# Gathered experts beside the late attention, and part of the dense experts' first products before the gates

## The chip, the cores and the metric

The kernel runs on one NeuronCore of a Trainium2 chip. The metric is the time of one launch on the device in microseconds (us); three runs of the kernel before gave 3617.83, 3618.16 and 3625.24, so the median is 3618.16.

## What is computed

One layer of a hybrid decoder, for 1024 prompt tokens (8 blocks of 128) and 32 sample tokens (8 sequences of 4 tokens, each with 2048 cached positions). A projection feeds an S5 state-space head group and latent attention; both are mixed and added to the input. Then comes PEER, a retrieval over 128 x 128 experts, which takes more than half of the time. Cut to that part:

```python
q = (xb @ wq).reshape(PEER_BLOCK, PEER_HEADS, 2, PEER_HALF)
s = jnp.einsum('qhcd,ckd->qhck', q, keys)
s1, i1 = lax.top_k(s[:, :, 0], PEER_TOPK)
s2, i2 = lax.top_k(s[:, :, 1], PEER_TOPK)
...
top, sel = lax.top_k(cand, PEER_TOPK)
idx = jnp.take_along_axis(cidx, sel, axis=-1)
g = jax.nn.softmax(top, axis=-1)
act = jax.nn.gelu(jnp.einsum('qhkd,qd->qhk', jnp.take(u_tab, idx, axis=0), xb))
return jnp.einsum('qhk,qhkd->qd', (g * act), jnp.take(v_tab, idx, axis=0))
```

Each token picks 128 of 16384 experts (8 heads x 16); expert number = first key x 128 + second key.

## The kernel before

The tokens are treated in two ways. Blocks 0 to 2 (`early`) and the sample block are *sparse*: `Sparse.block` gathers, slot by slot, 128 rows of `peer_u` (tile `pu`) by an indirect DMA from POOL, multiplies them with the tokens and sums them on DVE (`pact`), and later gathers `peer_v` rows (`pv`) and adds them into `pacc`. That is 2 x (3 x 128 + 32) = 832 gathers of 512 KB and as many DVE steps, with five row buffers (`RB`). Blocks 3 to 7 (`late`, 640 tokens, `TD`) are *dense*: every one of the 16384 experts is computed and weighted by a gate that is zero where the expert was not picked. `Gates` builds the gates in memory (`g_d`), 80 steps of 8 tokens; `Dense.group` then goes over the 128 second keys, four at a time: load and split `ur` into a high and a low part (`uh`, `ul`), 48 products of 320 columns (`da`, the first products), gelu, times the gate, split (`hh`, `hl`), and 30 products of 512 columns with the `peer_v` rows of that key (`dy`, `dres`).

Before that, in the program's order: S5 and projections; `attention` over all 64 units (block, head) with the 16 steps of `split_wq` (split the query weights and write them to `wq_d`) beside it; `mix_out` for all 8 blocks (`oz`); `score` for all 8 blocks (query products `rqp`, key products `rscp`, the best 16 by `top16` on DVE); `select` for the three early blocks, which makes the lists that the gathers need; then, in `rest`, `select` for the late blocks, the sample's attention (`Sample.run`: 8 sequences, key products `kk`, then `soften` and `gather`), the sample block's own mixing, scoring and selection between the gate steps, and the dense stage. `weave` puts the gathers between the steps of `rest`: each step yields a cost, cost x `PACE` is credit, and a gather step costs 1.5.

A scheduler of the language then reorders the instructions of each engine by its own estimate, within the dependencies and the buffers; each engine and each DMA queue (SP, ACT, POOL) then runs its list strictly in order. So sample work stands among the attention in the built program although it is written behind it.

Of the kernel before, what the change touches and what calls it, by code (L numbers as in the profile page):

```python
# [22 lines left out]
NB = 8  # L23
# [227 lines left out]
def build(ctx, nc, tc, a):  # L251
# [58 lines left out]
    xn_d = dram.tile([NT, D], F32, name="xn_d")  # L310
    g_d = dram.tile([NTB, 128, 128, TBLK], F32, name="g_d")
# [12 lines left out]
    es = ExitStack()  # L324
    with right():
        smp = Sample(es, nc, tc, a, ident, keep, o_d)
# [16 lines left out]
    sparse.open(ctx.enter_context(tc.tile_pool(name="ring", bufs=1)))
    er = ExitStack()
    slots = er.enter_context(tc.tile_pool(name="slots", bufs=1))
    i1T, wT = (slots.tile([128, TD], F32, name=nm) for nm in ("i1T", "wT"))
    i2T = slots.tile([128, TD], BF16, name="i2T")

    def take_dense(b, i1, i2, w, pool, pp):
        cs = slice((b - D0) * 128, (b - D0) * 128 + 128)  # L350
        tp = pp.tile([128, 3, 128], F32, name=f"slt{b}", tag="slt")
        for j, (src, dst) in enumerate(((i1, i1T), (i2, i2T), (w, wT))):
            nc.tensor.transpose(tp[:, j], src, ident)
            nc.scalar.copy(dst[:, cs], tp[:, j])

    e2 = ExitStack()
    pools = ranks(e2, nc, tc, a, "p")
    for b0, n in SSEL:
        select(nc, pools, early[b0 : b0 + n], tv[:, b0 : b0 + n], ti[:, b0 : b0 + n], sparse.take)

    def rest():

        for b0, n in DSEL:
            bs = slice(D0 + b0, D0 + b0 + n)
            select(nc, pools, late[b0 : b0 + n], tv[:, bs], ti[:, bs], take_dense)
            yield 25.0 * n
        e2.close()
        et.close()
        drive(smp.run())
# [1448 lines left out]
```

## Time and profile before

| what | value |
|---|---|
| median of three runs | 3618.16 us |
| the profiled execution: time / span | 3620.32 us / 3617.9 us |
| mean granted TensorE clock | 0.944 |
| PE busy | 3347.4 us, 93% |
| PEld (weight loads) busy | 2929.9 us, 81% |
| DVE / ACT / POOL busy | 2716.4 / 1156.2 / 1233.4 us |
| HBM traffic | 229 GB/s over the span |

The span is from the first to the last instruction; 2.4 us of the profiled time lie around it. PE's matmuls overlap each other, so its busy time is an upper reading of its work; start-to-start intervals in the timeline tell what one matmul really takes. The granted clock is a share of 2.4 GHz; 0.5 is 1.2 GHz.

### The profile page before, as it was taken

How to read it: one execution, taken by the hardware profiler on the slowest of the kernel's cores; microseconds unless marked ns; L12 is line 12 of the kernel's file. 1: busy time of each engine (PE TensorE's matmuls, PEld its weight loads, DVE VectorE, ACT ScalarE, POOL GpSimd, SP SyncE). 2: the span in 40 equal slices, each digit the busy share in tenths (PEclk: the TensorE clock that was granted, in tenths of full speed). 3: DMA queues.
4: the chain of work that ended last, by engine and by line, in shares of the span. 5: the costliest groups of instructions: out<-in, count | busy, mean ns of one | idle time of the engine just before them, and what ended most of it. 6: DMA issues, size and time to landing. Idle time of an engine off the chain costs nothing.

```text
span 3617.9 us, 52406 instructions
## 1 busy us (share of the span) xinstructions
PE 3347.4 (93%) x19464; PEld 2929.9 (81%) x19464; DVE 2716.4 (75%) x5777; ACT 1156.2 (32%) x2268; POOL 1233.4 (34%) x1044
## 2 busy tenths in 40 slices
PE   8899899999999634998799999999999999999999
PEld 7778687765799523987798898889988989998898
DVE  7674664434577998779688888888888888888884
ACT  4333454422322422456522121222222222222221
POOL 1020100000000104222155556555555556555551
PEclk9889799999999866778899999999999999999999
DMA  3335931143322207777899999999999999999992
GB/s 132 86 88 155 315 130 46 48 152 111 115 82 71 87 26 250 290 248 252 294 308 312 318 318 325 320 315 341 321 314 313 342 333 318 326 317 324 327 328 104
DMA packets 324606, 832.19 MB, mean 230 GB/s; under 512 B 36696, under 2 KB 150488, under 8 KB 313536
## 3 DMA queue, kind: packets, MB, share of 16 engines
q0 software_dynamic: 130608, 510.98, 39.9%
q1 hardware_dynamic: 92752, 247.75, 20.0%
q10 hardware_dynamic: 100992, 70.13, 6.7%
q8 instruction: 153, 2.51, 0.3%
q14 instruction: 101, 0.83, 0.1%
HBM read 734.44 MB, written 92.94 MB: 229 GB/s over the span
## 4 chain that ended last, share of the span: by engine, by line
PE 42%; issue 19%; POOL 13%; DMA 13%; DVE 11%; ACT 2%; SPq 0%; ACTq 0%; POOLq 0%; DVEq 0%
POOL pv L1335 9%; DMA pv<-in_peer_v_dram,idx 6%; POOL pu L1335 4%; PE gps L1219 4%; PE oz L1029 3%; DMA pu<-in_peer_u_dram,idx 2%; DVE pu L1349 2%; PE po L709 2%; PE s L688 2%; PE kk L139 2%; PE rqp L139 2%; PE rqp L140 2%; PE rqp L141 2%; PE kk L141 1%; PE kk L140 1%
## 5 line engine op out<-in xcount | busy, mean ns | idle before, releaser
L1335 POOL DMA_INDIRECT pu<-in_peer_u_dram,idx x384 | 522.6, 1361 | 618.3 <-DVE pact L1349 478.9
L1335 POOL DMA_INDIRECT pv<-in_peer_v_dram,idx x384 | 521.4, 1358 | 391.2 <-DVE pacc L1361 282.9
L139 PE MATMUL da<-xdh,uh 128*128 128x320 f32 x2048 | 636.8, 311 | 19.0 <-ACT ga L1292 18.7
L141 PE MATMUL da<-xdh,ul 128*128 128x320 f32 x2048 | 634.8, 310 | 2.3 <-DVE ul L129 2.3
L140 PE MATMUL da<-xdl,uh 128*128 128x320 f32 x2048 | 635.1, 310 | 0.0
L1361 DVE SCALAR_TENSOR_TENSOR pacc<-pv,pw,pacc 128x1024 f32<-128x1024 f32 x416 | 533.8, 1283 | 100.0 <-DMA pv<-in_peer_v_dram,idx 90.8
L1349 DVE CUSTOM_DVE_ANT_0 pu<-pu,pxn 128x1024 f32<-128x1024 f32 x416 | 496.7, 1221 | 90.2 <-DMA pu<-in_peer_u_dram,idx 82.5
L139 PEld LDWEIGHTS da<-xdh,uh 128*128 128x128 f32 x2048 | 387.1, 189 | 30.3 <-ACT ga L1292 23.5
L140 PEld LDWEIGHTS da<-xdl,uh 128*128 128x128 f32 x2048 | 387.1, 189 | 6.4
L141 PEld LDWEIGHTS da<-xdh,ul 128*128 128x128 f32 x2048 | 386.6, 189 | 6.3 <-DVE ul L129 2.8
L139 PE MATMUL dy<-vh,hh 128*128 128x512 f32 x768 | 302.5, 394 | 20.4 <-DVE yac L1308 20.4
L140 PE MATMUL dy<-vl,hh 128*128 128x512 f32 x768 | 299.8, 391 | 0.0
L141 PE MATMUL dy<-vh,hl 128*128 128x512 f32 x768 | 298.0, 390 | 0.0
L128 ACT CAST uh<-ur 128x1024 fp32r<-128x1024 f32 x128 | 134.5, 1051 | 394.3 <-PE da L140 391.3
L1292 ACT ACTIVATE ga<-da 128x320 f32<-128x320 f32 x256 | 110.0, 432 | 428.6 <-PE da L141 426.8
L1219 PE MATMUL gps<-hv,h 128*128 128x128 f32 x800 | 203.8, 415 | 23.8 <-DVE hv L1212 5.5
L128 ACT CAST vh<-vr 128x1024 fp32r<-128x1024 f32 x128 | 132.0, 1049 | 249.2 <-DMA vr<-in_peer_v_dram 180.0
L129 DVE TENSOR_TENSOR vl<-vr,vh 128x1024 fp32r<-128x1024 f32 x128 | 156.4, 1223 | 60.1 <-ACT vh L128 59.6
L1219 PEld LDWEIGHTS gps<-hv,h 128*128 128x128 f32 x800 | 168.8, 242 | 39.8 <-issue 16.4
L139 PE MATMUL dres<-vh,hh 128*128 128x512 f32 x512 | 200.5, 392 | 0.0
L140 PE MATMUL dres<-vl,hh 128*128 128x512 f32 x512 | 199.6, 392 | 0.0
L139 PEld LDWEIGHTS dy<-vh,hh 128*128 128x128 f32 x768 | 144.2, 188 | 54.5 <-DVE yac L1308 25.2
(528 smaller groups left out, 7148.1 us busy)
## 6 DMA issues: line engine op xcount, KB each, us to landing
ur<-in_ut_dram SPq DMA_DIRECT2D x128, 512.0 KB, 6.3
vr<-in_peer_v_dram SPq DMA_DIRECT2D x128, 512.0 KB, 6.5
g_d<-gbuf SPq DMA_DIRECT2D x20, 2048.0 KB, 7.6
gt<-g_d ACTq DMA_DIRECT2D x32, 1280.0 KB, 18.1
wq_d<-wq POOLq DMA_DIRECT2D x16, 1024.0 KB, 7.8
rwp<-wq_d POOLq DMA_DIRECT2D x16, 1024.0 KB, 5.1
rwn<-wq_d POOLq DMA_DIRECT2D x16, 1024.0 KB, 5.4
wqr<-in_peer_wq_dram SPq DMA_DIRECT2D x16, 512.0 KB
```

Of the source, the lines that this page charges most:

```text
L128: nc.scalar.copy(hi, raw)
L129: nc.vector.tensor_tensor(lo, raw, hi, OP.subtract)
L139: nc.tensor.matmul(out, ah, bh, start=(first and i == 0), stop=False)
L140: nc.tensor.matmul(out, ah, bl, start=False, stop=False)
L141: nc.tensor.matmul(out, al, bh, start=False, stop=(last and i == n - 1))
L688: nc.tensor.matmul(s[:, c0 : c0 + w], qT[:, h, :], kT[:, h, c0 : c0 + w], start=True, stop=c0 + w != nk)
L1029: nc.tensor.matmul(z[:n], cat[:, k, :n], w[:, k, hs], start=(k == 0), stop=(k == 7))
L1219: nc.tensor.matmul(ps[:, :, j - j0], h1[:, j], hv[:, :, j] if j < GV else ha[:, j - GV], start=True, stop=True)
L1292: nc.scalar.activation(ga[:, cs], ps[:, :HW], AF.Gelu_apprx_tanh)
L1335: self.nc.gpsimd.indirect_dma_start(out=r, out_offset=None, in_=self.a[table], in_offset=bass.IndirectOffsetOnAxis(ap=ix, axis=0))
L1349: nc.vector.tensor_tensor_reduce(ur, ur, xn, 1.0, 0.0, OP.mult, OP.add, act[:, s : s + 1])
L1361: nc.vector.scalar_tensor_tensor(acc, vr, w[:, s : s + 1], acc, OP.mult, OP.add)
```

## The change

Attention is still one generator over all blocks, but only the 24 units of the early blocks come first, with the 16 `split_wq` steps beside units 2 to 17. Mixing, scoring and selection of the three early blocks follow at once, and the gathers may start. The other 40 attention units, the mixing and scoring of the late blocks (the query weights and `w_out` are read once more) now stand in `rest`, with sample steps between them, and give credit for gathers. The gate steps give less credit (1.5 for 4.0), the dense steps too (2.16 for 2.35). New is `Ahead`: for 16 of the 128 second keys (7, 15, ... 127) the first products are made before the dense stage and written to `ad_d` in memory; the dense stage loads them (327,680 bytes a key) in place of `ur`, its split and 48 products. `Ahead` has one buffer of each kind. The diff, cut:

```diff
-    drive(attention(nc, tc, a, ident, qkv, o_d, early + late, lambda pool: split_wq(nc, a, pool, wq_d)))
-    drive(mix_out(nc, tc, a, gl_d, o_d, x1_d, xn_d, early + late, "e"))
...
-    drive(score(nc, tc, a, ident, xn_d, [(early, None), (late, xt)], lambda b: tv[:, b], lambda b: ti[:, b], "p", wq_d))
...
+    att = attention(nc, tc, a, ident, qkv, o_d, early + late)
+    next(att)
+    with right(), tc.tile_pool(name="wqs", bufs=2) as pool:
+        for _, _ in zip(split_wq(nc, a, pool, wq_d), range(16)):
+            next(att)
+    for _ in range(8 * D0 - 17):
+        next(att)
+    drive(mix_out(nc, tc, a, gl_d, o_d, x1_d, xn_d, early, "e", "right"))
+    with right(), ExitStack() as e1:
+        tv, ti = tops(e1, D0, "e")
+        drive(score(nc, tc, a, ident, xn_d, [(early, None)], lambda b: tv[:, b], lambda b: ti[:, b], "e", wq_d, 2, "right"))
+        pools = ranks(e1, nc, tc, a, "e")
+        for b0, n in SSEL:
+            select(nc, pools, early[b0 : b0 + n], tv[:, b0 : b0 + n], ti[:, b0 : b0 + n], sparse.take)
+    es = ExitStack()
+    with right():
+        smp = Sample(es, nc, tc, a, ident, keep, o_d)
...
+        short_att = smp.run()
...
+        for _ in beside(att, 1, ATT_FREE):
+            yield 15.0
+        for _ in beside(mix_out(nc, tc, a, gl_d, o_d, x1_d, xn_d, late, "d"), 2):
+            yield 40.0
...
+        for _ in beside(score(nc, tc, a, ident, xn_d, [(late, xt)], lambda b: tv[:, b - D0], lambda b: ti[:, b - D0], "d", wq_d), 1):
+            yield 5.0
+        ea = ExitStack()
+        ahead = Ahead(ea, nc, tc, a, xt, ad_d)
...
+                select(nc, pools, late[b0 : b0 + n], tv[:, bs], ti[:, bs], lambda *x: take_dense(dst3, *x))
+                for _ in range(3 * n):
+                    next(short_att, None)
         et.close()
-        drive(smp.run())
+        drive(short_att)
...
         for _ in gates:
-            yield GT * 0.5
+            yield 1.5
+        drive(ahead.run())
...
-DENSE_PACE = 2.35
+DENSE_PACE = 2.16
+ATT_FREE = 20
...
+AHEAD = list(range(7, 128, 8))
...
+class Ahead:
...
+        self.sp = es.enter_context(tc.tile_pool(name="ah", bufs=1))
+        self.pp = es.enter_context(tc.tile_pool(name="ahp", bufs=1, space=PSUM))
...
+        for n, i2 in enumerate(AHEAD):
+            ur = sp.tile([128, 8, 128], F32, name=f"aur{i2}", tag="ur")
+            nc.sync.dma_start(ur, self.a["ut"][i2])
+            uh = sp.tile([128, 8, 128], F32R, name=f"auh{i2}", tag="uh")
+            ul = sp.tile([128, 8, 128], F32R, name=f"aul{i2}", tag="ul")
+            split(nc, uh, ul, ur)
+            da = sp.tile([128, TD], F32, name=f"ada{i2}", tag="da")
+            for c0 in range(0, TD, HW):
+                cs = slice(c0, c0 + HW)
+                ps = self.pp.tile([128, 512], F32, name=f"aps{i2}_{c0}", tag="da")
+                mm3(nc, ps[:, :HW], [(uh[:, k], ul[:, k], xh[:, k, cs], xl[:, k, cs]) for k in range(8)])
+                nc.scalar.copy(da[:, cs], ps[:, :HW])
+            nc.sync.dma_start(self.ad_d[n], da)
...
+            if i2 in AHEAD:
+                nc.sync.dma_start(ga, self.ad_d[AHEAD.index(i2)])
+                nc.scalar.activation(ga, ga, AF.Gelu_apprx_tanh)
+            else:
```

What the scheduler makes of it, at three places. First DVE, where the sample's set-up stands (`qg`, `qTb`, `pidx`, `sukl`). Before, among the attention's maxima (`mx`) of the third block:

```order
L691 TENSOR_REDUCE mx_0_4806<-s_0_4803 128x1
L802 TENSOR_SCALAR qg<-qTs,gk 64x256
L815 COPY qTb<-qTs 96x256
L704 COPY pT_7_4810<-pt_7_0_4811 128x256
L691 TENSOR_REDUCE mx_1_4835<-s_1_4832 128x1
L723 TENSOR_TENSOR oT_4827<-oT_4827,po_4699 128x512
L691 TENSOR_REDUCE mx_2_4857<-s_2_4854 128x1
```

Now, straight behind the end of the early selection (`fi` and `idx` are the last early block's list; `pT_7` and `oT` belong to the last attention unit):

```order
L1393 SCALAR_TENSOR_TENSOR fi_6463<-kn_6443,kn_6453 128x128
L1394 CAST idx<-fi_6463 128x128
L831 TENSOR_SCALAR qg<-qTs,gk 64x256
L844 COPY qTb<-qTs 96x256
L736 COPY pT_7_8876<-pt_7_0_8877 128x512
L821 TENSOR_SCALAR pidx<-ptx 128x8
L822 TENSOR_TENSOR pidx<-pidx,ptx 128x8
L129 TENSOR_TENSOR sukl<-sukr,sukh 128x512
L129 TENSOR_TENSOR movl<-sukr,movh 128x2x256
```

The whole attention now stands ahead of the sample's set-up; before, half of the sample's work stood among it.

Second PE, around the last late selection (`slt` turns its results) and the first gate (`gps`). Before:

```order
L353 MATMUL slt_9676<-ident,re_9592 128x128
L353 MATMUL slt_9824<-ident,kn_9804 128x128
L353 MATMUL slt_9824<-ident,kn_9814 128x128
L353 MATMUL slt_9824<-ident,re_9765 128x128
L1070 MATMUL rtp_0_13998<-ident,rxn_13996 128x32 x4
L1070 MATMUL rtp_1_14005<-ident,rxn_13996 128x32 x4
L1219 MATMUL gps_0_13935<-hv_13927,h_0_13925 128x128 x4
L1219 MATMUL gps_4_13941<-hv_13927,h_0_13925 128x128
```

Now, the 768 products `aps` of `Ahead` stand among `kk` and `slt`, some 1100 rows ahead of the first gate:

```order
L141 MATMUL kk_1_0_11692<-sukh,sll_0_11526 128x256
L357 MATMUL slt_12729<-ident,kn_12684 128x128
L139 MATMUL aps_0_17069<-xdh,auh_17064 128x320
L140 MATMUL aps_0_17069<-xdl,auh_17064 128x320
...
L357 MATMUL slt_12729<-ident,kn_12703 128x128
...
L141 MATMUL aps_320_17095<-xdh,aul_17065 128x320
L357 MATMUL slt_13282<-ident,kn_13244 128x128
L139 MATMUL aps_0_17129<-xdh,auh_17124 128x320
L140 MATMUL aps_0_17129<-xdl,auh_17124 128x320
L141 MATMUL aps_0_17129<-xdh,aul_17125 128x320
```

Two keys follow each other there with one row between them, where the splits `auh` and `aul` have one buffer. The sample's last `kk` rows, `soften`, `gather` and `soa` stand behind the last `aps`, and the first `gps` behind them, as before.

Third SP's queue in the dense stage, where a key of `AHEAD` has its load:

```order
L1339 DMA vr_18450<-in_peer_v_dram 128x1024
L1339 DMA vr_18523<-in_peer_v_dram 128x1024
L1334 DMA ur_18792<-in_ut_dram 128x1024
L1339 DMA vr_18719<-in_peer_v_dram 128x1024
L1334 DMA ur_18868<-in_ut_dram 128x1024
L1339 DMA vr_18798<-in_peer_v_dram 128x1024
L1349 DMA ga_18531<-ad_d 128x640
L1334 DMA ur_18947<-in_ut_dram 128x1024
L1334 DMA ur_19196<-in_ut_dram 128x1024
```

`ga` is read back from memory in the same queue as `ur` and `vr`; in the kernel before nothing but those two stands here.

## Rows read from the trace of the kernel before

**Rows 1.** Stretches: start:end, length, busy PE PEld DVE ACT POOL, clock, DMA share, GB/s.
```profile
450.00:756.00 306.00, 305.04 (x2155) 242.33 (x2153) 157.69 (x276) 146.08 (x383) 11.78 (x21) 1.00 0.21 69
756.00:950.00 194.00, 181.37 (x811) 110.19 (x812) 73.97 (x211) 44.30 (x126) 6.91 (x12) 0.96 0.47 156
950.00:1180.00 230.00, 228.76 (x1589) 227.86 (x1588) 171.71 (x1027) 59.09 (x140) 7.99 (x15) 1.00 0.23 76
1180.00:1429.00 249.00, 111.29 (x692) 81.63 (x692) 235.43 (x1077) 78.67 (x166) 54.52 (x44) 0.70 0.35 118
1429.00:1640.00 211.00, 205.98 (x1111) 191.75 (x1112) 155.62 (x223) 106.63 (x231) 49.66 (x51) 0.77 0.73 262
1640.00:1783.00 143.00, 125.53 (x635) 117.05 (x633) 134.44 (x252) 91.18 (x188) 37.50 (x31) 0.86 0.75 269
1783.00:1812.00 29.00, 14.82 (x67) 14.55 (x68) 9.48 (x13) 7.29 (x10) 2.91 (x2) 0.66 0.87 275
1812.00:3618.00 1806.00, 1774.74 (x9875) 1607.10 (x9873) 1488.00 (x1758) 436.98 (x632) 1008.40 (x746) 1.00 0.90 312
```

**Rows 2.** Groups in 1180 to 1429 us: instructions, count, busy us, mean ns.
```profile
L1335 POOL DMA_INDIRECT pu<-in_peer_u_dram,idx x32 | 46.7, 1460 | 132.0 <-DVE pact L1349 106.8 <-DVE idx L1330 16.4 <-issue 6.7
L1349 DVE CUSTOM_DVE_ANT_0 pu<-pu,pxn 128x1024 f32<-128x1024 f32 x28 | 32.9, 1212 | 0.8 <-DMA pu<-in_peer_u_dram,idx 0.8
...
L880 DVE TENSOR_REDUCE ssq<-ssqr 128x8 f32<-128x512 f32 x28 | 18.9, 673 | 0.6 <-ACT ssqr L877 0.6
```

**Rows 3.** Timeline of PE, 2500 to 2506 us: start, us, instruction.
```profile
2499.95 0.32 PE L140 MATMUL da<-xdl,uh 128*128 128x320 f32 x1
...
2505.69 0.31 PE L140 MATMUL da<-xdl,uh 128*128 128x320 f32 x1
```

**Rows 4.** Timeline and chain that ended last: third attention block, the sample's set-up.
```profile
418.17 0.56 DVE L691 TENSOR_REDUCE mx<-s 128x1 f32<-128x384 f32 x1 [0.94 <-PE s L689]
...
416.98 14.54 DMA sukr<-in_w_uk_dram
437.99 2.12 PE qpp L808 x18
```

**Rows 5.** Tile wq and its write: ns min/median/max; KB, us from issue to landing.
```profile
L128 ACT CAST wq<-wqr x16: 1030/1050/1122, 368.6 to 488.7; 128x1024 fp32r<-128x1024 f32 x16
L129 DVE TENSOR_TENSOR wq<-wqr,wq x16: 1209/1216/1226, 371.0 to 490.3; 128x1024 fp32r<-128x1024 f32 x16
...
wq_d<-wq POOLq DMA_DIRECT2D x16, 1024.0 KB, 7.8
```

**Rows 6.** Timeline of PE in mixing and scoring; chain: products of one mixing block.
```profile
800.30 0.30 PE L140 MATMUL kk<-movl,slh 128*128 128x288 f32 x1
800.44 0.30 PE L141 MATMUL kk<-movh,sll 128*128 128x288 f32 x1
...
840.35 13.73 PE oz L1029 x32
...
1010.29 0.33 PE L141 MATMUL rqp<-rxhp,rwp 128*128 128x384 f32 x1
1010.46 0.61 PE L1091 MATMUL rscp<-keysp,rqTp 128*128 128x128 f32 x4
1010.82 0.42 PE L139 MATMUL rqp<-rxhp,rwp 128*128 128x384 f32 x1
```

**Rows 7.** Tile kk: first and last start.
```profile
L139 PE MATMUL kk<-sukh,slh x256: 277/282/682, 452.7 to 1284.8; 128*128 128x256 f32 x128
```

**Rows 8.** Groups in 1640 to 1783 us: gathered blocks on DVE.
```profile
L1349 DVE CUSTOM_DVE_ANT_0 pu<-pu,pxn 128x1024 f32<-128x1024 f32 x30 | 36.6, 1221 | 0.0
```

**Rows 9.** Stretches, tile pu (DVE, POOL, clock, DMA), then pacc (PE, PEld, DVE, POOL).
```profile
1812.00:3550.00 1738.00, 379.78 (x319) 438.07 (x316) 1.00 0.93 321
...
1812.00:3550.00 1738.00, 0.00 (x0) 0.00 (x0) 533.77 (x416) 3.87 (x6) 1.00 0.93 321
```

**Rows 10.** Waits in 1900 to 3400 us: us in total, times, longest.
```profile
DVE pacc L1361 <- DMA pv<-in_peer_v_dram,idx: 87.3, 79, 4.9
```

More of the change, by code (lines that the diff above doesn't have):

```diff
@@ L310, in build @@
     xn_d = dram.tile([NT, D], F32, name="xn_d")
+    ad_d = dram.tile([len(AHEAD), 128, TD], F32, name="ad_d")
     g_d = dram.tile([NTB, 128, 128, TBLK], F32, name="g_d")
@@ L323, in build @@
     sparse = Sparse(nc, tc, a, hold, x1_d, xn_d)
-    es = ExitStack()
-    with right():
-        smp = Sample(es, nc, tc, a, ident, keep, o_d)
+    sparse.open(ctx.enter_context(tc.tile_pool(name="ring", bufs=1)))
     wq_d = dram.tile([16, 128, 2, 8, 128], F32R, name="wq_d")
@@ L343, in build @@
[L343 to L349, printed above, removed]
+    att = attention(nc, tc, a, ident, qkv, o_d, early + late)
[3 more added lines that the diff above has]
+            next(att)
@@ L357, in build, with beside @@
-    pools = ranks(e2, nc, tc, a, "p")
-    for b0, n in SSEL:
-        select(nc, pools, early[b0 : b0 + n], tv[:, b0 : b0 + n], ti[:, b0 : b0 + n], sparse.take)
     def rest():
[L363 to L367, printed above, removed]
+        short_att = smp.run()
+        def beside(steps, n, first=0):
+            for i, _ in enumerate(steps):
+                if i >= first:
+                    for _ in range(n):
+                        next(short_att, None)
+                    yield
@@ new lines, in rest @@
+        ea = ExitStack()
+        ahead = Ahead(ea, nc, tc, a, xt, ad_d)
+        er = ExitStack()
+        slots = er.enter_context(tc.tile_pool(name="slots", bufs=1))
+        i1T, wT = (slots.tile([128, TD], F32, name=nm) for nm in ("i1T", "wT"))
+        i2T = slots.tile([128, TD], BF16, name="i2T")
+        dst3 = i1T, i2T, wT
+        with ExitStack() as e2:
+            pools = ranks(e2, nc, tc, a, "d")
+            for b0, n in DSEL:
+                bs = slice(b0, b0 + n)
+                select(nc, pools, late[b0 : b0 + n], tv[:, bs], ti[:, bs], lambda *x: take_dense(dst3, *x))
+                for _ in range(3 * n):
+                    next(short_att, None)
@@ L388, in rest @@
                 if next(gates, 1) is None:
-                    yield GT * 0.5
+                    yield 1.5
         for _ in gates:
-            yield GT * 0.5
+            yield 1.5
+        drive(ahead.run())
         with right():
-            dense_mm = Dense(ctx, nc, tc, a, ident, xt, g_d, x1_d)
+            dense_mm = Dense(ctx, nc, tc, a, ident, xt, g_d, x1_d, ad_d)
         eb.close()
         er.close()
+        ea.close()
         sparse.pp = dense_mm.pa
@@ L661, in split_wq, with attention @@
         yield
-def attention(nc, tc, a, ident, qkv, o_d, blocks, job, side="left"):
+def attention(nc, tc, a, ident, qkv, o_d, blocks, side="left"):
     with ExitStack() as e1, ExitStack() as e2:
@@ L759, in attention @@
                 close(b, po, rss[b])
-            if b >= 2:
-                next(extra, None)
             yield 0.5 + 0.55 * (b + 1)
@@ L1272, in group @@
             i2 = j0 + j
-            ur = xp.tile([128, 8, 128], F32, name=f"ur{i2}", tag="raw", bufs=UB)
-            nc.sync.dma_start(ur, a["ut"][i2])
-            uh = xp.tile([128, 8, 128], F32R, name=f"uh{i2}", tag="uh")
-            ul = xp.tile([128, 8, 128], F32R, name=f"ul{i2}", tag="ul")
-            split(nc, uh, ul, ur)
+            if i2 not in AHEAD:
+                ur = xp.tile([128, 8, 128], F32, name=f"ur{i2}", tag="raw", bufs=UB)
+                nc.sync.dma_start(ur, a["ut"][i2])
+                uh = xp.tile([128, 8, 128], F32R, name=f"uh{i2}", tag="uh")
+                ul = xp.tile([128, 8, 128], F32R, name=f"ul{i2}", tag="ul")
+                split(nc, uh, ul, ur)
             vr = xp.tile([128, 1024], F32, name=f"vr{i2}", tag="vr", bufs=VB)
```

31 lines of the change are left out of this document (18 added, 13 removed).

## The prediction

> **What bounds the kernel now.** I read the busy times by stretch first, then the groups of the costly stretches, the timeline of PE and the waits. The stretches [rows 1] show four limits in turn. From 450 to 1180 us PE is busy for nearly all of the time: 305 of 306 us in the attention, 181 of 194 in the mixing, 229 of 230 in the scoring. From 1180 to 1429 us lies a hole: PE is busy for 111 of 249 us, its granted clock falls to 0.70 between its two levels, and DVE is busy for 235. Here the late selection, the last sample keys and the first 28 gathered blocks [rows 2] all stand on DVE. The gates follow in two parts, 1429 to 1640 with PE busy for 206 of 211 us, and 1640 to 1783 with DVE busy for 134 of 143. Last comes the dense stage, 1806 us with PE busy for 1775 at clock 1.00, so there a PE product that goes away is time that goes away. What one costs is not its busy time, since products overlap: 40 `da` products start between 2499.95 and 2505.69 us [rows 3], 39 intervals in 5.74 us, so 0.147 us each, where each row alone says 0.31.
>
> The change drops no PE work. 768 products leave the dense stage and are done before it. So a gain can only come from time in which PE stands or crawls, and that is 138 us in the hole, 13 in the mixing, 17 in the second half of the gates, and the slow clock of hole and gates.
>
> **Start to the sample's set-up (367 to 759).** Blocks 0 and 1 run as before: the third block's first maximum comes at 418.2 [rows 4], so 50 us, or 25 a block and 3.1 a unit. Beside units 2 to 17 stand the 16 `split_wq` steps. One step takes cast 1.05, difference 1.22 and write 7.8 us [rows 5]; with 1 for its load that is 11 us, and two buffers give one step per 5.5 us, 88 us from 402, so to 490. That is 73 past 417. By the order list the early mixing comes with one more attention block: 3 x 13.73 [rows 6] + 25 = 66. The early scoring is 16 pieces of 24 query products (start to start 1010.29 to 1010.46, 0.17) and six key products (four take 0.36, so 0.09 each) [rows 6], 4.7 us a piece and 75 in all, with five attention units (17) among them, and about 10 for `xn` through memory: 102. The early selection is DVE work. In the hole DVE is busy for 235, less 33 for `pu` and 19 for `ssq` [rows 2], which leaves 23 a block for eight blocks with some sample work in it, so I take 20: 60, and 13 attention units beside it whose maxima and copies DVE does in the same list, 41: 101. Sum 50 + 73 + 66 + 102 + 101 = 392, to 759. In the kernel before this point was passed at 417 and the sample's keys began at 452.7 [rows 7], since its set-up stood among the attention.
>
> **From the set-up to the first gate (759 to 1479; before, the first gate stood at 1429).** PE has here: `kk`, 256 of each of six kinds, 1536, at 0.13 from start to start (800.30 to 800.44 is 0.14) [rows 6, 7], 200; five mixing blocks of 13.73, 69; 768 late query products of 0.147, 113; 160 key products of 0.09, 14; the `aps`, 16 x 48 x 0.147 = 113; some 640 small ones (turns, `soften`, the sample's own block) at 0.09, 58: 567. DVE has about as much. By the order list 117 gathers stand ahead of the first gate where there were 28: 117 x 1.21 [rows 2] = 142. The late scoring has five eighths of the 172 us of [rows 1], 107. Five selections of 20 are 100; `ssq` 128 x 0.673 [rows 2] = 86, and 44 for the split of the latents; the 16 splits of `Ahead` at 1.22 [rows 5], 20; and 65 for the rest: 564. Two lists of that length that wait for each other don't run at 1.0. The share of PE was 0.99 in the scoring, 0.93 in the mixing, 0.45 in the hole [rows 1]; I take 0.9, nearest the mixing, since DVE was 38% busy there and will be fuller here: 630. The ends of this are 573 (0.99) and 709 (0.8). Two stretches come on top. The set-up has nothing on PE beside it now: `sukr` takes 14.5 us to land, then `qpp`, then keys; from 417 to 452.7 it was 36 with attention as cover [rows 4, 7], so 30 (0 if late attention still covers, 36 if not). And the sample's last chain (`soften`, `gather`, `soa`, mixing, scoring) stands behind the last `aps` and has no cover: 60. That makes 720, so to 1479, 50 later than before, with 113 of moved products and 108 of moved DVE steps inside.
>
> **Gates and ramp (333 + 29).** The first part is PE's, 211 as before. In the second DVE sets the pace with 30 gathered blocks [rows 8]. The gate steps now earn less credit, and some 32 gathers stand in the stage instead of 66; so 17 of those 30 go: 17 x 1.22 = 21 of 143, leaving 122. Nothing less, since DVE was busy for 134 there. Then 29 of ramp as before [rows 1]: 1479 + 333 + 29 = 1841.
>
> **Dense (1693).** 768 products x 0.147 = 113 less than 1806. It has 683 gathers for 735, so DVE, at 82%, isn't the next bound: 319 `pu` and 416 `pacc` were 380 and 534 us of it [rows 9]. DMA is the near one, at 0.90; 52 gathers of 512 KB and 16 x 190 KB fall away, 30 of 563 MB or 5%, against 6% of the time, so its share rises to 0.91. If that pace bound, the stage would lose 92, not 113. The loads of `ga` go through SP's queue behind `ur` and `vr`; each has the group's second products as cover (a group is 1806/32 = 56 us, its first products 4 x 48 x 0.147 = 28, so 28 are left), and if one comes late the nearest row is a wait of 4.9 us, the longest for `pv` [rows 10].
>
> **Sum.** 1841 + 1693 = 3534 of span; with 2.4 around it 3536.4 against 3620.3 of the profiled execution, 83.9 less. From the median 3618.16 that is 3534. The 1841 are 29 more than 1812. With the ends above (573 to 709 for 630, 92 for 113) this case's own range is 3480 to 3600.
>
> **Rivals.** *The hole closes wholly.* If DVE and PE interleave without loss, the 175 us in which PE is not busy between 450 and 1783 (length less busy, summed) [rows 1] go: 3620 - 175 = 3445. For it: attention, keys and gathers are independent and now stand together. Against: DVE is then as full as PE. The Trainium skill (Perfetto Trace Analysis, Identifying the Most-Contended Engine) says that matmul busy time is a bad reading of headroom and that weight-load busy should be read instead. The rows bear that out in kind: in the same stretches loads are busy for 362 us less than the span, and by loads alone it would be 3620 - 362 = 3258; but the mixing, with DVE and ACT both lightly used, had loads at 110 of 194 us [rows 1], so most of this is not to be had, and I don't take it.
>
> *The read-back is late.* Should each `ga` hold PE for 4.9 us [rows 10], 78 of the 113 come back: 3612, no difference to speak of. Against it: its buffer is free early and it is 320 KB.
>
> *Slower: gathers hold DVE in the middle.* There 117 gathered steps stand in DVE's strict list between the sums `ssq`, the maxima and the selection, and PE's next keys wait behind those. In the dense stage a step whose row was not there waited for 87.3 us in 79 cases, 1.1 each [rows 10]. If each of the 117 waits as long, and `kk` behind it, 129 come on top: 3663. It decides from 84/117 = 0.72 us a gather. For it: POOL took 1.46 us to issue one in the hole [rows 2] and 438/316 = 1.39 in the dense stage [rows 9], and five buffers come free only by DVE. Against: in the hole 28 `pu` steps waited for 0.8 in all [rows 2]. The Trainium skill (SBUF — State Buffer, SBUF: two separate sides) has a rule that speaks against this change: a DMA issued from GpSimd has its descriptors written by GpSimd, and a Vector operation that holds the shared port locks it out for its whole length. By it the issue would grow where DVE is fullest, and the 1.46 beside DVE at 95% against 1.39 at 82% agrees in sign only, 0.07 us; the sum above has no term for it.
>
> *The change doesn't do what it says*: the scheduler's list could put the late attention so that the sample stands behind it and nothing covers it. The list shows that in part, and the terms hold it.
>
> **Chances.** Forecast 0.57; hole closed 0.13; late read-back 0.10; slower by the gathers 0.17; no effect 0.03. A measurement of this kernel can tell 0.2%, or 7 us, from no change. Faster: 0.57 + 0.13 + 0.06 of the read-back = 0.76; within: 0.04 + 0.02 = 0.06; slower 0.17 + 0.01 = 0.18. The range is 3440 to 3640: it takes in the closed hole and the read-back and the milder half of the slower case.
>
> **What would show it.** Right: `wq` casts some 5.5 us apart; PE idle for 30 us near 759; the first gate near 1479 with 117 `pu` steps ahead of it; clock near 1.0 from 1180 to the gates; 1693 us from the first `da` to the end. Wrong: waits of `pu` or of `ssq` and `mx` on DMA or DVE in the middle beyond 80 us, PE's share under 0.8 there, a wait of ACT for `ga` in every eighth key, a dense stage over 1720.

## The result, and the profile after

The changed kernel takes 3635.36 us (median of 15 runs, 3619.68 to 3649.94) against 3617.83 for the kernel before in the same series: ratio 1.0051, 95% interval [1.0036, 1.0067]. It is slower by half a per cent where 3534 was forecast. The profiled execution is the slowest of its 15, 3649.94 us with a span of 3648.2, so its places lie up to 14.6 us behind those of a median run.

The stretches of the changed kernel, the view of [rows 1] (start:end, length, busy PE, PEld, DVE, ACT, POOL, granted clock, DMA share, GB/s):

```profile
402.00:505.00 103.00, 74.86 (x296) 46.26 (x296) 41.09 (x57) 37.11 (x77) 8.77 (x16) 0.70 0.83 283
505.00:572.00 67.00, 62.19 (x206) 31.20 (x207) 16.74 (x45) 10.60 (x23) 1.08 (x2) 0.95 0.41 141
572.00:702.00 130.00, 127.27 (x766) 109.62 (x766) 76.36 (x382) 35.91 (x77) 8.59 (x16) 1.00 0.46 157
702.00:805.00 103.00, 82.27 (x417) 56.19 (x415) 91.21 (x433) 37.17 (x57) 4.88 (x5) 0.83 0.09 29
805.00:825.00 20.00, 12.26 (x79) 10.67 (x77) 6.15 (x14) 3.91 (x8) 4.79 (x7) 0.76 0.93 310
825.00:950.00 125.00, 115.57 (x485) 73.11 (x485) 74.88 (x173) 28.43 (x87) 35.12 (x29) 0.94 0.68 223
950.00:1005.00 55.00, 41.58 (x305) 36.85 (x303) 47.73 (x97) 23.50 (x66) 26.68 (x27) 0.86 0.90 332
1005.00:1220.00 215.00, 206.20 (x1538) 199.70 (x1538) 193.98 (x807) 66.34 (x188) 82.45 (x79) 0.97 0.65 228
1220.00:1490.00 270.00, 237.06 (x1723) 222.61 (x1723) 199.12 (x749) 111.62 (x265) 27.20 (x30) 0.92 0.31 104
1490.00:1571.60 81.60, 47.75 (x337) 36.92 (x337) 30.50 (x63) 21.43 (x59) 2.65 (x4) 0.75 0.28 95
1571.60:1913.00 341.40, 330.42 (x1729) 296.51 (x1728) 245.83 (x390) 199.66 (x422) 70.05 (x44) 0.87 0.57 213
1913.00:1942.00 29.00, 22.40 (x123) 21.07 (x124) 8.11 (x8) 9.54 (x14) 0.00 (x0) 0.88 1.02 349
1942.00:3648.00 1706.00, 1665.51 (x9098) 1495.50 (x9097) 1410.09 (x1663) 419.70 (x601) 959.26 (x695) 0.99 0.90 312
```

The dense stage did nearly what it should: 1706 us from 1942 to the end, where it had 1806. The time is lost ahead of it: 1942 us pass before that stage, against 1812. And the hole of [rows 1], 249 us with 138 without PE, is not closed; about as much time without PE now lies in six places: 28 us without PE from 402 to 505, 21 beside the early selection (702 to 805), 8 in the set-up, 13 from 950 to 1005, 33 beside the late selection (1220 to 1490), 34 ahead of the gates (1490 to 1571.6). In five of these six the mean granted clock is 0.70 to 0.86, so PE ran part of them at the lower of its two levels, 0.5.

The places that the forecast named, by tile (columns: ns shortest/median/longest, first to last start). `mx` are the attention's maxima, one per unit; `sukr` is the load that opens the sample's set-up. First three lines of the kernel before, where `kk` began at 452.7 [rows 7]:

```profile
L691 DVE TENSOR_REDUCE mx<-s x64: 278/754/1226, 367.6 to 730.6; 128x1 f32<-128x128 f32 x8, 128x1 f32<-128x256 f32 x8, 128x1 f32<-128x384 f32 x8, 128x1 f32<-128x512 f32 x8
...
L1219 PE MATMUL gps<-hv,h x800: 388/409/582, 1429.0 to 1781.0; 128*128 128x128 f32 x160
...
L129 DVE TENSOR_TENSOR hl<-ga,hh x128: 810/821/865, 1806.5 to 3588.9; 128x640 fp32r<-128x640 f32 x128
```

Then the changed kernel:

```profile
L723 DVE TENSOR_REDUCE mx<-s x64: 277/758/1225, 359.6 to 799.1; 128x1 f32<-128x128 f32 x8, 128x1 f32<-128x256 f32 x8, 128x1 f32<-128x384 f32 x8, 128x1 f32<-128x512 f32 x8
...
L128 ACT CAST wq<-wqr x16: 1032/1044/1046, 402.4 to 492.6; 128x1024 fp32r<-128x1024 f32 x16
...
L814 ACTq DMA_DIRECT2D sukr<-in_w_uk_dram x1: 432/432/432, 805.3 to 805.3; - x1
...
L139 PE MATMUL kk<-sukh,slh x256: 275/281/582, 824.4 to 1523.8; 128*128 128x256 f32 x128
...
L1248 PE MATMUL gps<-hv,h x800: 388/409/577, 1571.6 to 1911.5; 128*128 128x128 f32 x160
...
L129 DVE TENSOR_TENSOR hl<-ga,hh x128: 810/821/829, 1940.8 to 3620.3; 128x640 fp32r<-128x640 f32 x128
```

And what waited (us in total, times, longest), from answers for 402 to 830, 800 to 1572 and 1942 to 3648 us:

```profile
PE oz L1058 <- DMA woe<-in_w_out_dram: 5.2, 1, 5.2
...
DVE pu L1413 <- DMA pu<-in_peer_u_dram,idx: 14.2, 10, 3.1
...
ACT ga L1350 <- DMA ga<-ad_d: 53.9, 16, 6.3
```

DVE hardly waits for the rows of the early gathers: ten waits, 14.2 us together, for some 118 rows.

### The profile page after: what moved, and what is told of

It is laid out like the page before. It is cut to its first block, busy times and chain, and to the rows that moved or that the text cites. A ratio compares the mean times of both kernels' runs of the same rounds, so it can differ in the third digit from the quotient of the medians.

```text
span 3648.2 us, 52616 instructions
## 1 busy us (share of the span) xinstructions
PE 3380.9 (93%) x19464; PEld 2943.6 (81%) x19464; DVE 2706.2 (74%) x5778; ACT 1169.7 (32%) x2286; POOL 1272.4 (35%) x1060
## 4 chain that ended last, share of the span: by engine, by line
PE 42%; issue 17%; DVE 14%; DMA 14%; POOL 10%; ACT 1%; SPq 0%; ACTq 0%; POOLq 0%; DVEq 0%
POOL pv L1399 7%; DMA pv<-in_peer_v_dram,idx 6%; PE gps L1248 4%; PE oz L1058 4%; POOL pu L1399 3%; DVE pu L1413 2%; DMA pu<-in_peer_u_dram,idx 2%; PE da L139 2%; PE da L141 2%; PE da L140 2%; PE dy L139 2%; PE dy L140 1%; PE dy L141 1%; PE s L720 1%; PE po L741 1%
## 5 line engine op out<-in xcount | busy, mean ns | idle before, releaser
L1399 POOL DMA_INDIRECT pv<-in_peer_v_dram,idx x384 | 548.8, 1429 | 534.5 <-DVE pacc L1425 390.6
L139 PE MATMUL da<-xdh,uh 128*128 128x320 f32 x1792 | 555.2, 310 | 9.1 <-ACT ga L1356 6.1
L141 PE MATMUL da<-xdh,ul 128*128 128x320 f32 x1792 | 554.7, 310 | 0.5 <-DVE ul L129 0.5
L140 PE MATMUL da<-xdl,uh 128*128 128x320 f32 x1792 | 554.8, 310 | 0.0
L139 PEld LDWEIGHTS da<-xdh,uh 128*128 128x128 f32 x1792 | 337.6, 188 | 18.8 <-ACT ga L1356 7.8
L140 PEld LDWEIGHTS da<-xdl,uh 128*128 128x128 f32 x1792 | 337.8, 189 | 6.8
L141 PEld LDWEIGHTS da<-xdh,ul 128*128 128x128 f32 x1792 | 337.3, 188 | 5.6 <-DVE ul L129 1.7
L128 ACT CAST uh<-ur 128x1024 fp32r<-128x1024 f32 x112 | 117.8, 1051 | 380.9 <-PE da L140 370.4
L1356 ACT ACTIVATE ga<-da 128x320 f32<-128x320 f32 x224 | 96.4, 432 | 359.8 <-PE da L141 356.1
L141 PE MATMUL dres<-vh,hl 128*128 128x512 f32 x512 | 187.0, 393 | 3.2 <-DVE hl L129 3.0
```

Of the source, the lines that this page charges most:

```text
L128: nc.scalar.copy(hi, raw)
L139: nc.tensor.matmul(out, ah, bh, start=(first and i == 0), stop=False)
L140: nc.tensor.matmul(out, ah, bl, start=False, stop=False)
L141: nc.tensor.matmul(out, al, bh, start=False, stop=(last and i == n - 1))
L1356: nc.scalar.activation(ga[:, cs], ps[:, :HW], AF.Gelu_apprx_tanh)
L1399: self.nc.gpsimd.indirect_dma_start(out=r, out_offset=None, in_=self.a[table], in_offset=bass.IndirectOffsetOnAxis(ap=ix, axis=0))
```

## The experiments

The changed kernel is two changes: the new order with its early gathers, and the 16 keys ahead. Each was run alone. Every time below is a median beside runs of the kernel before on the same chip (3616 to 3619), except for E4 to E6, which ran once each.

### E1: the new order without the keys ahead

```diff
-AHEAD = list(range(7, 128, 8))
+AHEAD = []
```

> The changed kernel without its 16 keys ahead: AHEAD is empty, all 128 keys make their first products in the dense stage; the early gathers stay. The dense stage was 104 us shorter with the 16 keys (first to last gate product 1782 in the kernel before, 1679 in the changed one), so that should come back. Theory 1 (the products moved ahead are partly hidden in idle time of the stretch 1220 to 1490, which lost 61 us): the first gate comes 60 to 80 us earlier, the total is 25 to 45 us above the changed kernel, 3660 to 3680. Theory 2 (they all stand in the path there, and the loss lies with them): the first gate comes 105 us or more earlier and the total is within 10 us of 3635 or below. Theory 3 (they are wholly hidden, and the loss lies all with the early gathers): the first gate moves by under 20, the total is about 3735.

Measured: 3672.53 us, ratio 1.0151 [1.0115, 1.0186]. The first gate and the last steps (`hl`) of the dense stage:

```profile
L1248 PE MATMUL gps<-hv,h x800: 387/410/563, 1514.8 to 1853.1; 128*128 128x128 f32 x160
...
L129 DVE TENSOR_TENSOR hl<-ga,hh x128: 811/821/827, 1884.1 to 3638.3; 128x640 fp32r<-128x640 f32 x128
```

The gate comes 57 us earlier than with the keys (1514.8 against 1571.6), so of their 113 us of products about half was hidden: theory 1 by its total and nearly by the gate (60 was its lower end). Part of the 57 is spread from run to run (E4 and E5 show how much). The dense stage is 1754.2 from first to last `hl`, 75 longer than with the keys (1679.5) and 28 shorter than in the kernel before (1782.4). It holds 51 gathers fewer than that of the kernel before (687 for 738 behind the first `hl`), but the 28 cannot be put down to them: E6, with 128 keys and the same 738 gathers, takes 1768.0, and E5, with 805, takes 1814.9, of which PE stood for 48.5 at one waiting product (`psy`, see E2), so some 1766 without that wait.

### E2: the keys ahead without the new order

```diff
 sparse.open(ctx.enter_context(tc.tile_pool(name="ring", bufs=1)))
+ea = ExitStack()
+ahead = Ahead(ea, nc, tc, a, xt, ad_d)
...
+        drive(ahead.run())
         with right():
-            dense_mm = Dense(ctx, nc, tc, a, ident, xt, g_d, x1_d)
+            dense_mm = Dense(ctx, nc, tc, a, ident, xt, g_d, x1_d, ad_d)
...
```

The class `Ahead` and the branch for its keys in `Dense.group` are put in as in the change itself, but for the shared buffer that is named here:

> The kernel before with the 16 keys ahead alone: attention, mixing, scoring, gathers and paces as before, Ahead opened behind the gathers' ring (its result shares the buffer of the raw rows, for space). By theory 1 the products belong where PE stood: the hole from 1180 to 1429 us has 138 us without PE, they take 113, and DVE there has 14 us free for 20 us of splits. The first gate comes 10 to 45 us later than 1429, the dense stage is 104 shorter, the total 3525 to 3565. Rival, the products cost their full time also here (DVE's list holds them): 3610 to 3630. Rival, the read-back or the single buffer costs more than it did: a dense stage over 1730.

Measured: 3593.78 us, ratio 0.9939 [0.9916, 0.9962], faster than both kernels, but above the range of theory 1 and below that of the rivals.

```profile
L141 PE MATMUL aps<-xdh,aul x256: 302/309/636, 1199.1 to 1711.7; 128*128 128x320 f32 x128
...
L1224 PE MATMUL gps<-hv,h x800: 387/409/582, 1445.2 to 1818.4; 128*128 128x128 f32 x160
...
L129 DVE TENSOR_TENSOR hl<-ga,hh x128: 806/818/826, 1847.9 to 3559.6; 128x640 fp32r<-128x640 f32 x128
...
PE psy L1411 <- DVE pacc L1401: 47.4, 1, 47.4
```

Of the 768 products 504 stand ahead of the first gate and that gate comes only 16 later, as theory 1 has it; the other 264 run on among the gates, which take 21 longer (373.2 from the first to the last `gps` of `hv`, 352.0 in the kernel before). The dense stage is 1711.7 and not 1678. The last row points at a cause, which E9 tests: one product, `psy`, which closes the sparse sample block, stood in PE's list for 47.4 us until the last gathered row was summed, and all products behind it with it.

| us | old order | new order |
|---|---|---|
| 128 keys in the dense stage | 3617.83 | 3672.53 (E1) |
| 16 keys ahead | 3593.78 (E2) | 3635.36 |

The keys gain in both orders, 24 and 37 us; the new order costs in both, 55 and 42.

### E3: four buffers for the split query weights

```diff
-        w = pool.tile([128, 2, 8, 128], F32R, name=f"wq{m}", tag="wq", bufs=2)
+        w = pool.tile([128, 2, 8, 128], F32R, name=f"wq{m}", tag="wq", bufs=4)
```

> The changed kernel with four buffers for the split query weights wq where there were two (the raw rows keep theirs). Theory: the ring of two held the attention of 402 to 505 us at one unit per 5.8 us; with four the casts come 3 us apart, that stretch shortens by 35 to 45 us, and everything behind moves forward with it: 3590 to 3605. Rival: the attention without other work beside it is held by its own chain (products, maximum, exponential, turn), so at most 10 to 15 us go: 3620 to 3630. Rival: the write of wq by the POOL queue sets the pace (7.8 us landing each, and they share the way): no change.

Measured: 3646.79 us, ratio 1.0074 [1.0053, 1.0096]; no gain over 3635.36, where the theory had 3590 to 3605. The casts (by tile), the stretch and the wait of PE from 790 to 830:

```profile
L128 ACT CAST wq<-wqr x16: 1035/1044/1048, 399.8 to 476.4; 128x1024 fp32r<-128x1024 f32 x16
...
402.00:505.00 103.00, 73.92 (x315) 45.09 (x315) 39.78 (x57) 36.86 (x78) 8.78 (x16) 0.77 0.91 321
...
PE qpp L837 <- DMA wukT<-in_w_ukT_dram: 20.3, 1, 20.3
```

The casts come 5.1 us apart instead of 6.0, not 3: the stretch now has a DMA share of 0.91 at 321 GB/s. Most of the 16 us won there is kept to the end of the attention (last list `idx` at 791.3 for 805.0) and lost in the set-up, where `qpp` waits 20.3 us for its weights; `kk` begins at 829.8, 5 later than with two buffers. The first gate comes at 1575.7. So two more buffers bring 0.9 us a step and not 3; what holds the steps at 5.1 us, the transfers or something else, no run shows.

### E4 and E5: no gathers in the middle, with and without the keys ahead

```diff
-            yield 15.0
+            yield 0.0
...
-            yield 40.0
+            yield 0.0
...
-            yield 5.0
+            yield 0.0
...
-DENSE_PACE = 2.16
+DENSE_PACE = 2.52
```

E5 has `AHEAD = []` besides.

> The changed kernel with no credit for gathers in the late attention, mixing and scoring, so the 117 gathers ahead of the first gate fall to few, and the dense stage gives more credit (2.52 for 2.16). Read up to the first gate only, since the dense stage then has some 100 more. If DVE's list sets the pace from 805 to 1571 us, the gathered steps (117 of 1.22) go out of it and the first gate comes 100 to 140 us earlier than 1572. If the chains and PE set it, it comes 0 to 40 us earlier. The dense stage has DMA at 0.90 now and should grow: 100 gathers of 512 KB at its 312 GB/s are 168 us of transfer, of which 10% of 1706 was free, so the total is above 3635 in either case unless the gate comes 100 earlier.

> The changed kernel without the 16 keys ahead and without credit for gathers in the late attention, mixing and scoring: what is left of the change up to the first gate is the new order alone (early blocks through mixing, scoring and selection first, the sample behind the attention). Each of the two taken out by itself brought the first gate from 1572 to 1515 (57 us each). If these are two costs that add, the gate comes near 1458, still 29 later than the 1429 of the kernel before, and those 29 are the price of the order. If both only filled the same idle time, the gate stays at 1490 or later and the order itself costs 60 or more. If the order cost nothing, 1430 or earlier. The dense stage then has all the gathers and 128 keys: total 3700 or more, not the question.

Measured: 3718.59 and 3666.0 us (one execution each, and read up to the first gate). The gates by tile, E4 first, then E5:

```profile
L1248 PE MATMUL gps<-hv,h x800: 388/409/561, 1514.4 to 1848.2; 128*128 128x128 f32 x160
```

```profile
L1248 PE MATMUL gps<-hv,h x800: 388/409/562, 1458.2 to 1795.7; 128*128 128x128 f32 x160
```

E4's gate at 1514.4 lies 57 earlier, outside both ranges that were set (100 to 140 for DVE's list, 0 to 40 for the chains and PE). E5's stands at 1458.2, where the sum of both had put it. Read so, the 142.6 us by which the first gate came later than in the kernel before are 29 for the order, 57 for the gathers in the middle and 57 for the 16 keys.

These figures are less sharp than they look. PE's and DVE's lists of the four programs are the same up to the sample's set-up, and yet it stands at different times:

| run | set-up (`sukr`) | first gate | between |
|---|---|---|---|
| changed kernel | 805.3 | 1571.6 | 766.4 |
| E1, no keys ahead | 797.6 | 1514.8 | 717.1 |
| E4, no gathers in the middle | 795.7 | 1514.4 | 718.7 |
| E5, neither | 800.9 | 1458.2 | 657.3 |

Counted from the set-up on, the keys cost 49 (changed kernel less E1) or 61 (E4 less E5), for 113 us of products, so about half; the gathers cost 48 or 60, for 116 DVE steps of 1.22 us (118 stand ahead of the gate in the changed kernel, 2 in E4), 142 us, so about 40%. The 29 for the order is the difference of two single traces and carries some 10 us of such spread.

What carries the gathers' cost is shown in part only. In E4 PE stands for 31 us less between set-up and gate (74.9 for 106.2); of its waits those that end with DVE are 24 us less and those that end with a transfer 13 less, while those on ACT are 5 more. The rest of the 48 is PE's busy time, 16 less. So waits on DVE are the largest part that the rows name; what makes the waits on transfers longer is not shown.

E5's total, 3666.0, lies below the 3700 that was expected.

### E6: the sample behind the attention, nothing else

```diff
-        smp = Sample(es, nc, tc, a, ident, keep, o_d)
+        hold_p = eh.enter_context(tc.tile_pool(name="held", bufs=1))
+    held = hold_p.tile([128, 12800], F32, name="held")
...
 drive(attention(...))
+    nc.gpsimd.dma_start(held[:, 0:512]..., o_d[:, :, (NB - 1) * 128 : NB * 128]...)
+    eh.close()
+    with right():
+        smp = Sample(es, nc, tc, a, ident, keep, o_d)
```

> The kernel before with one thing changed: the sample's memory is held until the last attention block is in memory, so its set-up and keys stand behind the attention, as in the changed kernel; nothing else moves by hand. In the kernel before, 780 of the 1536 kk and some small products, about 126 us of PE work, ran beside the attention from 452 to 730. Theory (the attention alone is held by its own chain, and the sample was what filled it): the last maximum comes at most 40 us earlier than 730, and the first gate 60 to 110 us later than 1429. Rival (PE was the limit of that stretch, so the sample cost there what it costs anywhere): the last maximum comes 100 us or more earlier, and the first gate within 30 of 1429.

Measured: 3695.87 us (one execution). The attention's maxima and the gates by tile:

```profile
L697 DVE TENSOR_REDUCE mx<-s x64: 277/758/1225, 370.9 to 620.1; 128x1 f32<-128x128 f32 x8, 128x1 f32<-128x256 f32 x8, 128x1 f32<-128x384 f32 x8, 128x1 f32<-128x512 f32 x8
...
L1225 PE MATMUL gps<-hv,h x800: 388/409/561, 1499.3 to 1871.3; 128*128 128x128 f32 x160
```

Neither side is whole. The attention sped up by 110 us (last maximum at 620.1 for 730.6), as the rival has it: PE had been its limit. (By tile, 686 and not 780 `kk` ran there in the kernel before, 104 us of busy PE.) But the first gate came 70 later, as the theory has it: of the sample's 1536 key products 780 now run at 1180 to 1500 beside the selection, where 336 ran before. From the last maximum to the first gate the time grew by 181 us, for work that had held up the attention by 110.

The same rows give the price of an attention unit without the sample beside it: 48 units of blocks 2 to 7 from 419.8, the first maximum of block 2, to 620.1, so 4.2 us each.

### E7 to E10: a version that beats both

E7 has 8 keys in the old order, E8 16 keys with a little less credit, E9 16 keys with `psy` last, E10 16 keys with more credit.

```diff
-AHEAD = list(range(7, 128, 8))
+AHEAD = list(range(15, 128, 16))      (E7)
...
-DENSE_PACE = 2.35
+DENSE_PACE = 2.32                     (E8; 2.5 in E10)
...
         if b < NB:
             nc.gpsimd.dma_start(self.a["y_prompt"][rows, :], acc)
             return
+        yield 40.0                    (E9)
```

> As the kernel before with keys ahead, but 8 keys (15, 31, ... 127) for 16. With 16 the first gate came 16 later, the gates took 22 longer because products ran into them until 1711, and the first to the last gate product of the dense stage took 71 less. The 8 keys' 384 products, 56 us, all fit ahead of the first gate: gate 1429 to 1440, gates as before, dense 35 to 45 less: 3575 to 3595, so at or below the 16 keys. Rival: each key gains the same 1.4 us and 8 gain half of 22, about 3605.

> As the kernel before with 16 keys ahead, but the dense stage gives 2.32 of credit for 2.35, so the gathers end nearer the end of the stage. With 16 keys that stage had its DMA share at 0.94 and PE lost 85 us in it where it lost 52 before. If the transfers' rate is what it loses to, a gather rate 1.3% lower gives back 5 to 15 us: 3580 to 3589. Rival: the last gathers now end so late that their sums stand behind the last products: 3595 to 3610.

> As the kernel before with 16 keys ahead, with the two products that close the sparse sample block (psy, which need its last sum) placed behind the last product of the dense stage. With 16 keys PE stood 47.4 us at psy, since the gathers ended later against PE's list than planned, and everything in its list behind them stood too; the kernel before has no such wait. If that wait is what kept 16 keys from their 104 us, the dense stage is 1665 to 1680 from its first to its last gate product and the total 3594 less 35 to 47, 3547 to 3560. Rival: the transfers hold the stage (share 0.94 in it), so the time only moves to other waits: 3580 to 3600.

> As the kernel before with 16 keys ahead, with 2.5 of credit for 2.35 in the dense stage, so that the gathers are issued some 6% denser. If they lag only because their credit is too small for the shorter stage, the wait at psy goes and the total is 3550 to 3570. If their rate is held by the transfers, the wait at psy stays or grows, as psy stands earlier too: 3590 to 3620.

| | us | ratio to before | first to last `hl` | wait at `psy` |
|---|---|---|---|---|
| E2 | 3593.78 | 0.9939 [0.9916, 0.9962] | 1711.7 | 47.4 |
| E7 | 3584.94 | 0.9896 [0.9871, 0.9920] | 1726.0 | none |
| E8 | 3605.35 | 0.9962 [0.9947, 0.9978] | 1718.5 | 42.8 |
| E9 | 3559.02 | 0.9830 [0.9801, 0.9858] | 1660.6 | 9.6 |
| E10 | 3674.53 | 1.0144 [1.0119, 1.0168] | 1793.1 | 134.4 |

E7 shows the dense stage without that wait:

```profile
L1224 PE MATMUL gps<-hv,h x800: 388/409/583, 1446.0 to 1803.9; 128*128 128x128 f32 x160
...
L129 DVE TENSOR_TENSOR hl<-ga,hh x128: 805/818/897, 1828.6 to 3554.6; 128x640 fp32r<-128x640 f32 x128
```

384 products fewer, 56.4 us by 0.147 each, and 56.4 us less than 1782.4 (that it fits to the digit is luck, with stages that differ by some 10 us from run to run). The total lies in the range of the expectation, though with a later gate and a shorter dense stage than it said. E7's first gate is 17 later, like that of E2 with twice the keys; E8's, whose list is that of E2 up to there, stands at 1456.1, so some 10 of this is the spread from run to run. E8's first theory failed and the range of its rival holds: with 1.3% less credit the last sum came 24 us later (3552.8 for 3529.1; 15 later counted from the first `hl`), and the wait stayed. E10 the other way, by the rival:

```profile
L1401 DVE SCALAR_TENSOR_TENSOR pacc<-pv,pw,pacc x416: 1269/1282/1325, 1934.2 to 3510.8; 128x1024 f32<-128x1024 f32 x139
...
PE psy L1411 <- DVE pacc L1401: 134.4, 1, 134.4
```

With 6% more credit the planned list puts `psy` some 580 products earlier, but the last sum came only 18 us earlier (3510.8 for 3529.1), so PE waited 134.4. With more credit the gathers' rate hardly followed (6% denser would bring the last sum some 100 us forward, of the 1681 us from the first `hl` to it in E2). E9 shows what the wait costs: against E2 the only edit is the place of the two products that make `psy` (four rows in the trace), and PE's list is that of E2 up to its last 364 rows. The last line is E2's for the same stretch:

```profile
L129 DVE TENSOR_TENSOR hl<-ga,hh x128: 810/818/826, 1852.0 to 3512.5; 128x640 fp32r<-128x640 f32 x128
...
1870.00:3520.00 1650.00, 1633.07 (x8947) 1473.13 (x8946) 1428.94 (x1707) 411.96 (x591) 1001.54 (x732) 1.00 0.94 332
...
PE psy L1412 <- DVE pacc L1401: 9.6, 1, 9.6
...
1870.00:3520.00 1650.00, 1592.05 (x8708) 1432.68 (x8706) 1427.83 (x1698) 404.89 (x578) 1005.84 (x737) 0.99 0.94 332
```

The dense stage is 1660.6, 122 less than before and 9 more than the 113 of its products, with the same 0.94 of DMA share from 1870 to 3520 us as E2 has (second and last line), while PE is busy for 41 us more of that stretch. So at this share the transfers did not hold the 51 us between E2 and E9; the wait did. The same wait stood in E4 (147.7 us) and E5 (48.5), and not in the kernel before, the changed kernel or E1. At 3559.02 it is the fastest version of this study, 59 us below the kernel before.

## Why the prediction was wrong

Two terms ahead of the dense stage failed, by 46 us each: the early scoring, 139 us for 102, which makes up most of the first 46, and PE's work from the sample's set-up to the first gate, 660 us for 567. The dense stage itself came nearly as forecast. Term by term:

- **The bound and the dense stage** were read rightly, and the size nearly: forecast 1693, measured 1706, and from first to last `hl` 103 less where 113 was expected. The keys alone give 75 by E1 and 122 by E9. That the gathers which left the stage had a part in the 103 is not shown: with 16 keys the stage is 1679.5 with 687 gathers behind the first `hl` and 1660.6 with 738 (E9).
- **The read-back** of `ga` waits for memory 16 times, 53.9 us on ACT, and PE hardly feels it: the rival that priced it at 78 fell.
- **"Start to the sample's set-up (367 to 759)"** failed by 46: the set-up stood at 805.3. The `wq` casts ended where forecast (492.6 for 490). What was mis-sized is the early scoring, "75 in all, with five attention units (17) among them, and about 10 for `xn` through memory: 102". Four stretches of the changed kernel in the view of [rows 1], then two of them by tile `mx` (columns: length, busy DVE and ACT with counts, clock, DMA share, GB/s):

```profile
507.00:569.00 62.00, 59.19 (x189) 29.28 (x189) 15.10 (x40) 9.43 (x21) 1.08 (x2) 0.96 0.39 131
569.00:599.00 30.00, 27.27 (x163) 18.58 (x162) 16.53 (x34) 13.21 (x28) 1.06 (x2) 1.00 0.52 184
599.00:708.00 109.00, 109.00 (x658) 97.70 (x657) 66.25 (x378) 24.81 (x53) 7.52 (x14) 1.00 0.42 142
708.00:805.00 97.00, 76.27 (x381) 51.45 (x379) 86.43 (x408) 36.21 (x55) 4.88 (x5) 0.82 0.09 31
...
569.00:599.00 30.00, 5.47 (x6) 5.77 (x12) 1.00 0.52 184
599.00:708.00 109.00, 7.67 (x8) 7.33 (x14) 1.00 0.42 142
```

The mixing, 507 to 569, took 62 for 66, the selection, 708 to 805, 97 for 101, and the mixing began at 507.4 for 490 (a wait of 5.2 for `woe` is in that). The scoring took 139 for 102: 30 us pass before its first query product at 599.4, and 14 attention units stand in it, not five. With PE busy for all of the 109 us of its products, each unit is time; a unit without the sample beside it takes 4.2 us by E6, where the sum took 3.1 to 3.4, a price of blocks 0 and 1, the shortest. The row of `mx` could have told that, 278 ns the shortest and 1226 the longest. Up to 10 of the 46 are spread: E4, with the same lists up to there, has its set-up at 795.7.
- **From the set-up to the first gate (759 to 1479)** failed by 46 again, 766 us for 720. The set-up took 19 for 30 (first `kk` at 824.4), the stretch up to the last `aps`, at 1489.1, 665 for 630, and the sample's last chain 82 for 60. The share "I take 0.9" was not what failed: from 825 to 1490 us PE is busy for 600 of 665 by the stretches in the section on the result, 0.90, in the reading by which the forecast had its shares. What failed is the sum of PE's work, "567": from set-up to gate PE is busy for 660 and stands for 106, where 567 in 720 would have left 153. The "some 640 small ones" are 1059 by count in the trace; `kk` was taken at 0.13 where its own row said 0.14; and the granted clock is below 1.00 in each of the six stretches, where the prices came from rows at 1.00.
- **What was moved** came out nearly right in sum, by luck. The formula charges the keys 113/0.9 = 126 us and the gathers nothing on top; E1, E4 and E5 show 49 to 61 for the keys and 48 to 60 for the gathers, 109 together. So the miss lies in the rest: without both, the forecast's own terms give (567 - 113)/0.9 + 30 + 60 = 594, and E5 has 657.
- **Gates and ramp**: 341 and 29 for 333 and 29. From the first gate to the first `hl` 27 gathered steps stand, where 66 stood and 32 were forecast; the gates are 13 shorter, not 21.
- **The slower rival** came out by its sign, but neither by its mechanism nor by its size (48 to 60 for 129). It had the gathered steps wait for their rows, 1.1 us each; they waited for 14.2 us in all. The largest part of their cost that E4 names is PE's waits on DVE, 24 us. The rule named beside it (the Trainium skill, SBUF — State Buffer, SBUF: two separate sides) would have the issue of a gather grow where DVE is fullest. POOL, by tile `pu`, for 805 to 1005 and 1005 to 1220 us (columns: length, busy DVE, busy POOL, clock, DMA share, GB/s):

```profile
805.00:1005.00 200.00, 57.97 (x49) 57.63 (x49) 0.90 0.77 261
1005.00:1220.00 215.00, 65.35 (x55) 67.72 (x55) 0.97 0.65 228
```

57.63/49 is 1.18 us an issue beside DVE at 64%, 67.72/55 is 1.23 beside DVE at 90%; in the kernel before it was 1.46 at 95% [rows 2] and 1.39 in the dense stage [rows 9]. These means hide what single rows of the changed kernel show:

```profile
847.06 1.67 POOL L1399 DMA_INDIRECT pu<-in_peer_u_dram,idx  x1 [1.60 <-DVE pact L1413]
849.00 1.22 DVE L1413 CUSTOM_DVE_ANT_0 pu<-pu,pxn 128x1024 f32<-128x1024 f32 x1
849.03 1.99 POOL L1399 DMA_INDIRECT pu<-in_peer_u_dram,idx  x1 [0.30 <-issue]
852.57 0.94 POOL L1399 DMA_INDIRECT pu<-in_peer_u_dram,idx  x1 [0.30 <-issue]
...
1158.31 4.39 POOL L1399 DMA_INDIRECT pu<-in_peer_u_dram,idx  x1 [0.30 <-issue]
```

A gather issue that begins while DVE stands, as at 852.57, takes 0.94 us (126 cases in the whole run, 0.93 to 1.00; spans on POOL are a rough reading, but these repeat). One that begins inside a `pu` step, as at 849.03, mostly ends 0.8 us after that step does (849.00 + 1.22 + 0.8 = 851.02): 1.62 us in the mean of 166 cases. Inside `pacc`, `ul` and `vl`, which also read two tiles in SBUF, it is the same; inside `ssq`, which reads one, and `yac`, one of whose two lies in PSUM, it stays at 0.94 (12 and 71 cases). The issue at 1158.31 lasted through three whole `pu` steps that followed each other without a gap. So an issue is held up while a DVE step reads two tiles in SBUF, as the rule has it for a step that holds the shared port; the kind of step counts, and not DVE's share. It is not what the early gathers cost, since DVE waited only 14.2 us for their rows.
- **The closed hole** (3445) was far off. Its premise, that the 175 us without PE were free for other work, is what E1, E4 and E5 deny: what goes into them costs some 40 to 50% of its time there, and in the old order a third (E2: 16 us at the gate and 21 in the gates, for 113).
- **The range**: the bounds that the sum names itself, 709 for 630 and 92 for 113, add 79 and 21 and end at 3634, not at the 3600 that it gives; the measured 3635 lies at that end.

In sum the forecast had 1841 us up to the dense stage and 1942 came: 46 in the first part, 46 in the second, 8 in the gates. The 13 in the dense stage are no more than the 14.6 us by which the profiled run lies above the median.

## What to carry to other kernels

Idle time of one engine is no account to book work on: while another list is nearly full, moved work costs a share of its own length (here some 0.4 for DVE steps, 0.3 to 0.5 for PE products), and work that was moved away from its cover has to find a new one (E6: the first gate 70 us later). A forecast of such a stretch needs every product in its list counted, the small ones too, before a share is put on it. Change two things together only after each has been priced alone; here one gained 24 to 37 us and the other lost 42 to 55. And look, after work has been taken out of a long stage, for an instruction in its list that waits for a slower stream: its place was planned for the longer stage, and moving it was worth 35 us (E2 to E9), more than the 24 that the keys had given without it.

## What the runs showed that was not expected

A single waiting product holds its engine's whole list: 47.4 us in E2 and 134.4 in E10, in a stage whose DMA share was 0.94 in E2 and in which PE's other waits that the rows name come to 21 us there. The stream of gathers did not speed up with its credit: 6% more brought its end forward by 18 us. Nor did the stage get shorter with fewer gathers in it: 1679.5 us with 687 of them, 1660.6 with 738 (E9), both with 16 keys. And the issue of a gather on POOL, 0.94 us by itself, waits out a DVE step that reads two tiles in SBUF, up to 4.39 us for one issue ahead of the first gate; why a stream of gathers ends up only 18 us earlier with 6% more credit, by this or by the transfers, stays open.
